# Stage 1 of a hybrid encoder block as a pipeline of 12 units, with inverse roots computed in rows

## The chip, the cores and the metric

The kernel runs on one core of one Trainium2 chip. The metric is device microseconds (us) of one execution, as the median over runs. TensorE (PE) multiplies matrices, VectorE (DVE), ScalarE (ACT) and GpSimd (POOL) work on tiles in SBUF, and SyncE (SP) issues nearly all transfers. Each engine executes its own instructions strictly in order, and waits on semaphores for the others.

## The reference

One layer over 1040 tokens (16 meta tokens and 1024 inputs), width 1024, all in float32:

```python
h = h + hybrid_mixer(rms_norm(h, norm_mix), w_in, ...)   # projections, two branches, gates, output
h = h + conv_ffn(rms_norm(h, norm_ffn), ffn_up, ffn_conv, ffn_down)
# hybrid_mixer, cut:
proj = hn @ w_in                                          # q, k, v, f_logit, rw, gates
qh, kh = rms_norm(q heads), rms_norm(k heads)             # forgetting attention, 8 heads of 64
z = rw + mu * (rw_prev - rw)                              # token shift for the RWKV-7 branch
kk = (kr * k_k) / max(norm per head, 1e-12)               # inverse root
y = rwkv7_scan(r, decay, k, v, -kk, kk * a)               # delta rule, done in 17 chunks of 64 tokens
yn = (y - mean) * rsqrt(var + GN_EPS)                     # per head
g_fox, g_rwkv = split(sigmoid(gates + g_b))
merged = g_fox * (o_fox @ w_bf) + g_rwkv * (o_rwkv @ w_br)
return merged @ w_o
```

## The kernel before, in words

Features lie on the 128 partitions and tokens along the free dimension, so a projection tile is [128 features, up to 384 tokens]. Tokens are cut in three groups `G` (384, 384, 272) in stage 1 and three windows `CW` of 342 later. Large products are split in a high and a low part of reduced float32 (`mm3`, lines 190 to 200: three matmuls per 128-row slice of the contraction); small ones are plain float32, which the records show as two instructions. Weights come through `wload` (L172): a transfer to `wf`, a cast on ACT to `wh`, a subtraction on POOL to `wl`, with `fb` and `wb` places.

An instruction scheduler orders each engine's list at build time: the order in which the source emits instructions is the priority, and an instruction of lower priority can go ahead where the scheduler's model sees the engine free. Tiles with one tag share a fixed number of places (`bufs`); a new tile waits until a place is released.

Stage 0 (`stage0`) loads and normalizes the input per group. Stage 1 (`stage1`) prepares the RWKV branch for four pairs of heads, `p` = 0 to 3. Per pair it emits the projections `zk`, `zr`, `zv` for all three groups (`proj`, `rw_tile`), the low-rank parts (`lora`), three units (`unit(p, c)`, one for each group), and `solve(p)`. A unit is a chain: a scan for the cumulated decay, exponentials, the normalized `kk` (L396 to L410: a block-sum matmul with `bo`, maximum, Ln, Exp, one Newton step of four instructions in `newton_rsqrt`), then `ar` and `bk`, the products `am` (L424) with their mask (L425), transposes of `bk` and `zv`, the bonus term, and stores. `solve` (L253) inverts triangular blocks: 128 instructions of transposing matmuls (L264), 60 dependent DVE steps (L275, L277) with matmuls back (L282), and two small rounds (L294, L301); its result `at` goes to `t_d` in memory. All temporaries and projections of stage 1 share one tag `u` with 28 places.

Gate projections (`gates`, L815) are a generator of 3-matmul steps, 16 weight tiles by three windows by eight steps, which `fill` advances between other work; each is placed behind `S.last_pe`, the last marked matmul on PE. At the end of stage 1 `fill(S, 84)` emits 92 steps. Stage 2 merges attention (`qk_chunk` normalizes queries and keys, one chunk ahead of its use) with the RWKV chain over 17 chunks (`rw_chain`) and, behind it, `group_norm`. Stage 3 multiplies the branches by their output weights and the gates (tanh of stored gate values, L940), stage 4 applies `w_out` and the second norm, stage 5 is the gated MLP.

Inverse roots: stage 0 takes Sqrt on ACT and a reciprocal on rows of tokens; `unit`, `qk_chunk`, `group_norm` and stage 4 work at full width, with the same sum in all rows of a head, by Ln and Exp(-0.5 x) on ACT and (not for queries) `newton_rsqrt`. PSUM tags in stage 1: three banks for projections, two for `aux`, two for `am` and `tp`, one for gates.

Of the kernel before, what the change touches and what calls it, by code (L numbers as in the profile page):

```python
# [7 lines left out]
F32 = mybir.dt.float32  # L8
F32R = mybir.dt.float32r
BF16 = mybir.dt.bfloat16  # L10
AF = mybir.ActivationFunctionType
# [27 lines left out]
NU = 28  # L39
# [15 lines left out]
def constants(S):  # L55
# [10 lines left out]
    S.eps = cp.tile([P, 1], F32, name="eps")  # L66
    nc.vector.memset(S.eps[:], NORM_EPS)
    S.geps = cp.tile([P, 1], F32, name="geps")
    nc.vector.memset(S.geps[:], GN_EPS)
# [3 lines left out]
def constants2(S):  # L73
# [9 lines left out]
    S.a0h = lin("a0", 4, 0.5, 0.0)  # L83
    S.kah = lin("k_a", 4, 0.5, 0.0)
# [17 lines left out]
def stage0(S, p0):  # L102
# [11 lines left out]
    for c, (t0, t1) in enumerate(G):  # L114
# [7 lines left out]
        else:  # L122
            tl = [U("xt") for _ in range(KD)]
# [6 lines left out]
    def stats(c):  # L130
# [12 lines left out]
        blk = [(a, min(P, n - a)) for a in range(0, n, P)]  # L143
        for j, (a, m) in enumerate(blk):
            for k in range(na):
                nc.tensor.matmul(ps[:m, j:j + 1], lhsT=sq[k][:, a:a + m], rhs=S.ones[:, 0:1], start=k == 0, stop=k == na - 1)
        r = p0.tile([P, 3], F32, name="r", bufs=2)
        for j, m in ((slice(0, 2), P), (slice(2, 3), blk[2][1])):
            nc.scalar.activation(out=r[:m, j], in_=ps[:m, j], func=AF.Sqrt, bias=S.eps[:m])
            nc.vector.reciprocal(out=r[:m, j], in_=r[:m, j])  # L150
        ps = psum(S, "tp")
        for j, (a, m) in enumerate(blk):
            nc.tensor.matmul(ps[:, a:a + m], lhsT=r[:m, j:j + 1].broadcast_to([m, P]), rhs=S.ident[:m, :m], start=True, stop=True)
# [18 lines left out]
def wload(S, src, kt, pool=None, tag="w", fb=3, wb=4):  # L172

    nc = S.nc
    pool = pool or S.wp
    res = []
# [130 lines left out]
def stage1(S):  # L307
    nc, tc = S.nc, S.tc
    with tc.tile_pool(name="p1", bufs=1) as p1:
        U = lambda name: p1.tile([P, 390], F32, name=name, tag="u", bufs=NU)  # L310
        v3 = lambda t, nc_: t[:, :64 * nc_].rearrange("p (c t) -> p c t", t=64)
# [3 lines left out]
        tc.keep_in_program_order(nc.scalar.preload_act_table_set("sqrt_and_others"))  # L315
# [8 lines left out]
        for c in stage0(S, p1):  # L324
# [6 lines left out]
            zk0.append(U("zk"))  # L331
# [6 lines left out]
        def proj(p, i):  # L338
            w = wload(S, S.A["w_rw"][2 + 3 * p + i], KD)
            z = []  # L340
            for c, (t0, t1) in enumerate(G):
                z.append(U(("zk", "zr", "zv")[i]))
                rw_tile(S, p1, 2 + 3 * p + i, z[c][:, :t1 - t0], w, c)
            pads(z[2])
            return z

        def lora(p, c):
# [3 lines left out]
            sw, tha = U("sw"), U("tha")  # L351
            ps = psum(S, "aux")
            nc.tensor.matmul(ps[:, :n], lhsT=lup[0:64, pc], rhs=wa[0:64, t0:t1], start=True, stop=True)
            with tc.issue_after(S.last_exp.ins) if p else nullcontext():
                nc.scalar.activation(out=sw[:, :n], in_=ps[:, :n], func=AF.Tanh, scale=0.5, bias=S.w0h[:, p:p + 1])
            ps = psum(S, "aux")
            nc.tensor.matmul(ps[:, :n], lhsT=lup[64:128, pc], rhs=wa[64:128, t0:t1], start=True, stop=True)
            with tc.issue_after(S.last_exp.ins) if p else nullcontext():
                S.th = nc.scalar.activation(out=tha[:, :n], in_=ps[:, :n], func=AF.Tanh, scale=0.5, bias=S.a0h[:, p:p + 1])
# [10 lines left out]
        def unit(p, c, zk, zr, zv, sw, tha, at):  # L370
# [18 lines left out]
            with tc.issue_after(S.ld.ins):  # L389
# [15 lines left out]
            if c == 2:  # L405
                nc.gpsimd.memset(inv[:, n:N], 1.0)
# [769 lines left out]
```

## Time and profile before

| | |
|---|---|
| median of 3 runs (range) | 2078.41 us (2077.85 to 2081.44) |
| profiled execution | 2079.23 us, span 2077.4 us, mean granted PE clock 0.954 |
| busy PE, PE weight loads | 1944.7 us, 1735.0 us |
| busy DVE, ACT, POOL | 901.8 us, 774.1 us, 563.7 us |

Busy times are of the profiled execution. In rows by stretch the columns are: start and end in us, length, then busy us and instruction count of PE, PE's weight loads, DVE, ACT and POOL, then the granted clock as a share of full speed, the busy share of the DMA engines and GB/s. In rows of waits: who waited, for whom, total us, times, longest. In rows of groups: line, engine, operation, tiles, shapes, count, busy us, mean ns, idle time before them. In rows of the timeline and the chain: start, duration, engine and line.

### The profile page before, as it was taken

Reading aid. Unit: us, or ns where it says so; the run is one execution under the profiler, and the core shown is the slowest. Engines: PE = TensorE matmul, PEld = TensorE weight load, DVE = VectorE, ACT = ScalarE, POOL = GpSimd, SP = SyncE. Lnnn points to the kernel's source line nnn. Section 1 sums busy time; section 2 is a strip of 40 time slices with the busy share of each in tenths; the row PEclk is TensorE's granted clock in tenths of the full one; section 3 lists DMA queues with packets and bytes.
Section 4 is the critical chain, followed back from the end, with each engine's and each line's share of the span. In section 5 each row is a group of like instructions: output and inputs, shape, how many; then the busy total and the mean of one; then the engine's idle time right before and its main releaser. Section 6 shows DMA issues by size and latency. Waiting matters only on the chain.

```text
span 2077.4 us, 34698 instructions
## 1 busy us (share of the span) xinstructions
PE 1944.7 (94%) x13800; PEld 1735.0 (84%) x13800; DVE 901.8 (43%) x1797; ACT 774.1 (37%) x1658; POOL 563.7 (27%) x614
## 2 busy tenths in 40 slices
PE   6969696996999999989989999899999999999999
PEld 5948575885888888877877999799898998999997
DVE  5156565554334244167343544843233332333333
ACT  5423242431454354267444534533132231322321
POOL 5311111120320131143221233533232232332322
PEclk9969797996999999999989999999999999999999
DMA  4131414141443233223102533211111111111112
GB/s 151 62 106 43 124 36 128 36 144 52 142 122 92 88 114 106 65 77 97 43 28 84 163 119 112 91 56 47 36 56 51 36 51 51 41 56 47 41 47 101
DMA packets 129489, 163.22 MB, mean 79 GB/s; under 512 B 20272, under 2 KB 87008, under 8 KB 129072
## 3 DMA queue, kind: packets, MB, share of 16 engines
q1 hardware_dynamic: 129072, 160.94, 25.5%
q8 instruction: 109, 1.79, 0.4%
q14 instruction: 52, 0.43, 0.1%
q0 software_dynamic: 256, 0.07, 0.0%
HBM read 117.49 MB, written 43.47 MB: 77 GB/s over the span
## 4 chain that ended last, share of the span: by engine, by line
PE 86%; DVE 7%; ACT 3%; DMA 2%; issue 1%; POOL 0%; SPq 0%; DVEq 0%; ACTq 0%; POOLq 0%
PE mm L196 15%; PE mm L198 15%; PE mm L197 15%; PE dn L196 4%; PE dn L198 4%; PE dn L197 4%; PE gate L196 3%; PE gate L197 3%; PE gate L198 3%; PE t L775 2%; PE o L789 2%; PE am L424 2%; PE s L740 1%; PE am L282 1%; PE s L741 1%
## 5 line engine op out<-in xcount | busy, mean ns | idle before, releaser
L184 POOL TENSOR_TENSOR wl<-wf,wh 128x512 fp32r<-128x512 f32 (+1 forms) x268 | 346.6, 1295 | 794.4 <-ACT wh L183 767.5
L197 PE MATMUL mm<-x,wh 128*128 128x344 f32 (+1 forms) x1056 | 339.1, 321 | 0.0
L196 PE MATMUL mm<-x,wh 128*128 128x344 f32 (+1 forms) x1056 | 337.6, 320 | 1.1 <-DVE ug L1014 1.0
L198 PE MATMUL mm<-x,wl 128*128 128x344 f32 (+1 forms) x1056 | 337.4, 320 | 1.0 <-POOL wl L184 1.0
L183 ACT CAST wh<-wf 128x512 fp32r<-128x512 f32 (+1 forms) x268 | 164.0, 613 | 379.5 <-PE dn L197 185.2
L196 PE MATMUL mm<-xh,wh 128*128 128x386 f32 (+5 forms) x624 | 211.2, 340 | 2.7 <-ACT xh L164 1.3
L198 PE MATMUL mm<-xh,wl 128*128 128x386 f32 (+5 forms) x624 | 210.2, 337 | 0.0
L197 PE MATMUL mm<-xl,wh 128*128 128x386 f32 (+5 forms) x624 | 209.4, 336 | 0.0
L196 PEld LDWEIGHTS mm<-x,wh 128*128 128x128 f32 x1056 | 199.2, 189 | 1.9 <-ACT uv L1012 1.2
L198 PEld LDWEIGHTS mm<-x,wl 128*128 128x128 f32 x1056 | 199.0, 189 | 1.7 <-POOL wl L184 1.6
L197 PEld LDWEIGHTS mm<-x,wh 128*128 128x128 f32 x1056 | 199.3, 189 | 0.4
L196 PE MATMUL gate<-xh,wh 128*128 128x342 f32 x384 | 139.4, 363 | 2.9 <-ACT sg L829 2.8
L1041 DVE TENSOR_TENSOR h<-h,dn 128x512 f32<-128x512 f32 x96 | 66.1, 689 | 168.9 <-PE dn L198 168.4
L198 PE MATMUL dn<-gh,wl 128*128 128x512 f32 x352 | 138.8, 394 | 0.0
L196 PE MATMUL dn<-gh,wh 128*128 128x512 f32 x352 | 138.6, 394 | 0.0
L197 PE MATMUL dn<-gl,wh 128*128 128x512 f32 x352 | 138.6, 394 | 0.0
L196 PEld LDWEIGHTS mm<-xh,wh 128*128 128x128 f32 x624 | 120.8, 194 | 10.0 <-issue 3.6
L197 PEld LDWEIGHTS mm<-xl,wh 128*128 128x128 f32 x624 | 120.9, 194 | 5.0 <-issue 1.6
L198 PEld LDWEIGHTS mm<-xh,wl 128*128 128x128 f32 x624 | 120.5, 193 | 5.3 <-issue 2.3
L198 PE MATMUL gate<-xh,wl 128*128 128x342 f32 x384 | 124.3, 324 | 0.0
L197 PE MATMUL gate<-xl,wh 128*128 128x342 f32 x384 | 124.2, 323 | 0.0
L1013 DVE SCALAR_TENSOR_TENSOR uv<-mm,par,uv 128x342 f32<-128x342 f32 (+1 forms) x66 | 37.8, 573 | 162.6 <-ACT uv L1012 162.6
(309 smaller groups left out, 3790.6 us busy)
## 6 DMA issues: line engine op xcount, KB each, us to landing
wf<-in_w_up_dram SPq DMA_DIRECT2D x88, 256.0 KB, 2.5
am<-am_d SPq DMA_DIRECT2D x17, 512.0 KB, 5.0
sg_d<-sg SPq DMA_DIRECT2D x48, 171.0 KB, 2.5
sg<-sg_d SPq DMA_DIRECT2D x48, 171.0 KB, 3.0
wf<-in_w_gate_dram SPq DMA_DIRECT2D x32, 256.0 KB, 2.8
wf<-in_w_out_dram SPq DMA_DIRECT2D x32, 256.0 KB, 2.9
wf<-in_w_down_dram SPq DMA_DIRECT2D x32, 256.0 KB, 2.7
am_d<-am SPq DMA_DIRECT2D x20, 384.0 KB, 2.9
```

What stands on the lines that cost most here:

```text
L183: nc.scalar.copy(out=wh[:, :n], in_=wf[:, :n])
L184: nc.gpsimd.tensor_tensor(out=wl[:, :n], in0=wf[:, :n], in1=wh[:, :n], op=ALU.subtract)
L196: nc.tensor.matmul(ps, lhsT=wh, rhs=xh, start=first and k == 0, stop=False)
L197: nc.tensor.matmul(ps, lhsT=wh, rhs=xl, start=False, stop=False)
L198: ins = nc.tensor.matmul(ps, lhsT=wl, rhs=xh, start=False, stop=last and k == n - 1)
L282: nc.tensor.matmul(ps[32 * k:32 * k + 32, n * t:n * t + n], lhsT=x[:nl, :, t0 + t], rhs=S.ident[:nl, 64 * k:64 * k + n], start=True, stop= ...
L424: nc.tensor.matmul(ps[:, j * P:(j + 1) * P], lhsT=bk[r, b0 + j, :], rhs=ar[r, b0 + j, :], start=True, stop=True)
L740: nc.tensor.matmul(ps, lhsT=q1[e][:, qs], rhs=k1[e][:, a:z], start=True, stop=False)
L775: S.last_pe = nc.tensor.transpose(ps[:r, (2 * j + e) * 116:(2 * j + e) * 116 + nq], pb[e][i][:nq, k:k + r], S.ident[:nq, :nq])
L789: S.last_pe = nc.tensor.matmul(po[64 * e:64 * e + 64, :nq], lhsT=vt[:r, kb, 64 * e:64 * e + 64], rhs=pt[:r, 2 * j + e, :nq], start=kb == 0 ...
L1013: nc.vector.scalar_tensor_tensor(out=t[:, :n], in0=ps[:, 1:1 + n], scalar=cw(1), in1=t[:, :n], op0=ALU.mult, op1=ALU.add)
L1041: nc.vector.tensor_tensor(out=hs, in0=hs, in1=ps[:], op=ALU.add)
```

## The change

Stage 1 is emitted as 12 units. Projections and LoRA are done per unit (`proj(p, c)`, `lora(p, c)`), one unit ahead of `unit(p, c)`; the three weight tiles of a pair are held over its three units; `solve(p - 1)` is emitted behind the first unit of pair `p`. Projections and LoRA tiles get a tag of their own, `z`, with 10 places; `u` keeps 15. The shifted projection is built in place, without `zt`. Orderings for ACT's table sets are dropped.

All inverse roots go through `rsqrt_rows`: sums are taken with the tile as stationary operand, so that tokens lie on partitions and the result has one or two columns per block of up to 128 tokens; a first guess from the bits of the float and four Newton steps run on these few columns; matmuls with the identity spread the result over the head's rows, into the same PSUM bank, from which it is read. Ln and Exp of all roots go away, the Sqrt of stage 0 too.

The gates take their tanh when they are stored, not in stage 3. The weight pool is opened three times (stage 1 with `wb` = 6, stage 2 with 4, from stage 3 on again); the last opens after the pool of the gates is closed. Three gate weight tiles, not four, use the common pool.

```diff
@@ stage1 @@
-        for p in range(NP_):
-            zk = proj(p, 0) if p else zk0
-            zr = proj(p, 1)
-            lo = [lora(p, c) for c in range(3)]
-            with tc.issue_after(S.th.ins):
-                S.ld = nc.scalar.preload_act_table_set("natural_log_exp_and_others")
-            zv = proj(p, 2)
-            at = p1.tile([64, 2 * NCH, 64], F32, name="at", bufs=2)
-            for c in range(3):
-                unit(p, c, zk[c], zr[c], zv[c], *lo[c], at)
-            solve(S, p1, p, at)
+        steps = [(p, c) for p in range(NP_) for c in range(3)]
+        def ahead(p, c):
+            return proj(p, c), lora(p, c)
+        ats = {}
+        nxt = ahead(0, 0)
+        for i, (p, c) in enumerate(steps):
+            (z, lo) = nxt
+            if c == 0:
+                ats[p] = p1.tile([64, 2 * NCH, 64], F32, name="at", bufs=2)
+            unit(p, c, *z, *lo, ats[p])
+            if c == 0 and p:
+                solve(S, p1, p - 1, ats[p - 1])
+            if i + 1 < len(steps):
+                nxt = ahead(*steps[i + 1])
+        solve(S, p1, NP_ - 1, ats[NP_ - 1])
...
+        def proj(p, c):
+            t0, t1 = G[c]
+            if c == 0:
+                S.wz = [wload(S, S.A["w_rw"][2 + 3 * p + i], KD) for i in range(1 if p == 0 else 0, 3)]
+            z = [zk0[c]] if p == 0 else []
+            for i in range(len(z), 3):
+                z.append(Z(("zk", "zr", "zv")[i]))
+                rw_tile(S, p1, 2 + 3 * p + i, z[i][:, :t1 - t0], S.wz[i - (p == 0)], c)
...
@@ unit @@
-            nc.tensor.matmul(ps[:, :n], lhsT=S.bo[:], rhs=kk[:, :n], start=True, stop=True)
-            inv = U("inv")
-            tn = U("tn")
-            ss = U("ss")
-            nc.vector.tensor_scalar(out=ss[:, :n], in0=ps[:, :n], scalar1=1e-24, scalar2=None, op0=ALU.max)
-            with tc.issue_after(S.ld.ins):
-                nc.scalar.activation(out=inv[:, :n], in_=ss[:, :n], func=AF.Ln)
-                S.last_exp = nc.scalar.activation(out=inv[:, :n], in_=inv[:, :n], func=AF.Exp, scale=-0.5)
-            newton_rsqrt(nc, inv[:, :n], ss[:, :n], 0.0, tn[:, :n])
+            inv = psum(S, "aux")
+            rsqrt_rows(S, p1, inv, [kk], n, S.bo[:, 0:P:64], 2, floor=1e-24)
...
+def rsqrt_rows(S, pool, ps, sq, n, ind, w, eps=None, floor=None):
+    nc = S.nc
+    nb = -(-n // P)
+    while n % nb:
+        nb += 1
+    m = n // nb
+    o = 496
+    for j in range(nb):
+        for i, q in enumerate(sq):
+            nc.tensor.matmul(ps[:m, o + w * j:o + w * j + w], lhsT=q[:, j * m:j * m + m], rhs=ind, start=i == 0, stop=i == len(sq) - 1)
+    W = w * nb
+    vt, yt, tt = [pool.tile([P, 8], F32, name=nm, bufs=2) for nm in ("rv", "ry", "rt")]
+    v, y, t = vt[:m, :W], yt[:m, :W], tt[:m, :W]
...
+    nc.vector.tensor_scalar(out=y.bitcast(I32), in0=v.bitcast(I32), scalar1=-0.5, scalar2=1597463007.0, op0=ALU.mult, op1=ALU.add)
+    for _ in range(4):
+        nc.vector.tensor_tensor(out=t, in0=v, in1=y, op=ALU.mult)
+        nc.vector.scalar_tensor_tensor(out=t, in0=t, scalar=-0.5, in1=y, op0=ALU.mult, op1=ALU.mult)
+        nc.vector.scalar_tensor_tensor(out=y, in0=t, scalar=1.5, in1=y, op0=ALU.add, op1=ALU.mult)
+    for j in range(nb):
+        for i in range(w):
+            r = P // w
+            l = yt[:m, w * j + i:w * j + i + 1].broadcast_to([m, r])
+            nc.tensor.matmul(ps[i * r:(i + 1) * r, j * m:(j + 1) * m], lhsT=l, rhs=S.ident[:m, :m], start=True, stop=True)
...
@@ qk_chunk (keys and queries), and alike in group_norm and stage4 @@
-    nc.tensor.matmul(pm[:, :n], lhsT=S.bo64[:], rhs=sq[:, :n], start=True, stop=True)
-    r = ap.tile([P, 348], F32, name="rq", bufs=1)
-    nc.scalar.activation(out=r[:, :n], in_=pm[:, :n], func=AF.Ln, bias=S.eps[:])
-    nc.scalar.activation(out=r[:, :n], in_=r[:, :n], func=AF.Exp, scale=-0.5)
-    if newton:
-        newton_rsqrt(nc, r[:, :n], pm[:, :n], NORM_EPS, ap.tile([P, 348], F32, name="rq2", tag="sq", bufs=1)[:, :n])
-    nc.vector.scalar_tensor_tensor(out=raw[:, :n], in0=raw[:, :n], scalar=gain, in1=r[:, :n], op0=ALU.mult, op1=ALU.mult)
+    rsqrt_rows(S, ap, pm, [sq], n, S.bo64[:, 0:P:64], 2, eps=NORM_EPS)
+    nc.vector.scalar_tensor_tensor(out=raw[:, :n], in0=raw[:, :n], scalar=gain, in1=pm[:, :n], op0=ALU.mult, op1=ALU.mult)
...
@@ gates, stage3 @@
-            nc.scalar.activation(out=sg[:], in_=ps[:, :342], func=AF.Identity, bias=S.par("gate_b", m))
+            nc.scalar.activation(out=sg[:], in_=ps[:, :342], func=AF.Tanh, scale=0.5, bias=S.gbh[:, m:m + 1])
...
-                nc.scalar.activation(out=sg[:], in_=sg[:], func=AF.Tanh, scale=0.5)
...
@@ build @@
-        S.wp = ctx.enter_context(tc.tile_pool(name="w", bufs=1))
         with tc.tile_pool(name="gp", bufs=1) as S.gp:
-            with tc.tile_pool(name="ps1", bufs=1, space=PSUM) as S.pp:
+            S.wb = 6
+            with tc.tile_pool(name="w1", bufs=1) as S.wp, tc.tile_pool(name="ps1", bufs=1, space=PSUM) as S.pp:
...
-            with tc.tile_pool(name="ps2", bufs=1, space=PSUM) as S.pp:
+            S.wb = 4
+            with tc.tile_pool(name="w2", bufs=1) as S.wp, tc.tile_pool(name="ps2", bufs=1, space=PSUM) as S.pp:
                 stage2(S)
+        S.wp = ctx.enter_context(tc.tile_pool(name="w3", bufs=1))
```

More of the change, by code (lines that the diff above doesn't have):

```diff
@@ L38 @@
 G = [(0, 384), (384, 768), (768, 1040)]
-NU = 28
+NU = 15
+NZ = 10
 _PCOLS = {}
@@ L122, in stage0 @@
         else:
-            tl = [U("xt") for _ in range(KD)]
+            tl = [U("xt") if c == 1 else p0.tile([P, 384], F32, name="xt", tag="z", bufs=NZ) for _ in range(KD)]
             for k in range(KD):
@@ L142, in stats @@
         ps = psum(S, "aux")
[L143 to L153, printed above, removed]
+        rsqrt_rows(S, p0, ps, sq[:na], n, S.ones[:, 0:1], 1, eps=NORM_EPS)
         return ps
@@ L169, in stage0, with wload @@
         yield c
-def wload(S, src, kt, pool=None, tag="w", fb=3, wb=4):
+def wload(S, src, kt, pool=None, tag="w", fb=3, wb=None):
     nc = S.nc
     pool = pool or S.wp
+    wb = wb or S.wb
     res = []
@@ L247, in rw_tile @@
     mm3(S, ps[:, :n + 2], w, xwin(S, t0, n + 2), mark=True)
-    t = pool.tile([P, 384], F32, name="zt", bufs=2)
-    nc.scalar.activation(out=t[:, :n], in_=ps[:, 2:2 + n], func=AF.Identity, scale=mu1)
-    nc.vector.scalar_tensor_tensor(out=z, in0=ps[:, 1:1 + n], scalar=mu, in1=t[:, :n], op0=ALU.mult, op1=ALU.add)
+    nc.scalar.activation(out=z, in_=ps[:, 2:2 + n], func=AF.Identity, scale=mu1)
+    nc.vector.scalar_tensor_tensor(out=z, in0=ps[:, 1:1 + n], scalar=mu, in1=z, op0=ALU.mult, op1=ALU.add)
 def solve(S, p1, p, at):
@@ L664, in attention @@
         n = t1 - t0
-        kn = qk_chunk(S, ap, wk, S.par("kg"), t0, t1, True)
+        kn = qk_chunk(S, ap, wk, S.par("kg"), t0, t1)
         for e in range(2):
@@ L791, in q_block @@
             yield 1.0
-    lb = ap.tile([P, 116], F32, name="lb", tag="rq", bufs=1)
+    lb = ap.tile([P, 116], F32, name="lb", bufs=1)
     nc.scalar.copy(out=lb[:, :nq], in_=po[:, 128:128 + nq])
@@ L858, in group_norm @@
             ps = psum(S, "gn")
-            nc.tensor.matmul(ps[:, :342], lhsT=S.bo64[:], rhs=sq[:], start=True, stop=True)
-            r = T("r", 2)
-            nc.scalar.activation(out=r[:], in_=ps[:, :342], func=AF.Ln, bias=S.geps[:])
-            nc.scalar.activation(out=r[:], in_=r[:], func=AF.Exp, scale=-0.5)
-            newton_rsqrt(nc, r[:], ps[:, :342], GN_EPS, sq[:])
-            nc.vector.tensor_tensor(out=y[:], in0=y[:], in1=r[:], op=ALU.mult)
+            rsqrt_rows(S, op, ps, [sq], 342, S.bo64[:, 0:P:64], 2, eps=GN_EPS)
+            nc.vector.tensor_tensor(out=y[:], in0=y[:], in1=ps[:, :342], op=ALU.mult)
             nc.scalar.activation(out=y[:], in_=y[:], func=AF.Identity, scale=S.par("gn_w", p), bias=S.par("gn_b", p))
@@ L994, in stage4 @@
                 st = psum(S, "st")
-                nc.tensor.matmul(st[:, :342], lhsT=S.ones[:], rhs=acc[c][:], start=True, stop=True)
+                rsqrt_rows(S, p4, st, [acc[c][:]], 342, S.ones[:, 0:1], 1, eps=NORM_EPS)
                 norm(c, st)
```

64 lines of the change are left out of this document (24 added, 40 removed).

## The prediction

> **What bounds the kernel now.** I read the 40 slices of the page first, then busy time by stage, then the waits of TensorE, then single rows for prices.
>
> ```profile
> PE   6969696996999999989989999899999999999999
> DVE  5156565554334244167343544843233332333333
> PEclk9969797996999999999989999999999999999999
> ```
>
> A slice is 52 us. TensorE (PE) is busy 9 tenths or more from slice 11 on, nearly without a break; the holes lie in the first ten, and in the same slices the granted clock falls. So stage 1 is the loose stage and all that follows is bound by PE. The stretches below give busy us (and counts) of PE, PE's weight loads, DVE, ACT and POOL, then the granted clock:
>
> ```profile
> 47.00:104.00 57.00, 57.00 (x333) 52.17 (x332) 11.29 (x21) 26.03 (x53) 24.48 (x35) 1.00 0.18 56
> 104.00:156.50 52.50, 33.07 (x154) 24.25 (x154) 29.41 (x51) 12.67 (x27) 8.55 (x16) 0.64 0.36 109
> 156.50:258.90 102.40, 85.18 (x727) 67.62 (x728) 59.01 (x127) 34.40 (x65) 18.20 (x32) 0.83 0.27 81
> 258.90:361.40 102.50, 85.47 (x727) 67.33 (x726) 59.24 (x127) 34.56 (x65) 17.87 (x32) 0.83 0.27 81
> 424.50:477.00 52.50, 47.82 (x310) 42.29 (x312) 24.32 (x41) 18.09 (x38) 13.74 (x20) 1.00 0.47 145
> 477.00:526.00 49.00, 30.62 (x433) 23.35 (x433) 23.59 (x66) 9.54 (x19) 4.18 (x12) 0.62 0.21 55
> 600.00:850.00 250.00, 248.56 (x2494) 211.96 (x2493) 92.87 (x223) 105.32 (x266) 45.67 (x47) 1.00 0.35 103
> ...
> PE am L424 <- DVE bk L415: 37.4, 7, 8.1
> PE am L282 <- DVE x L277: 11.8, 26, 1.0
> ```
>
> 47 to 104 us: projections, dense at full clock. 104 to 156.5: the three units of head pair 0, a chain of small steps on DVE; PE waits and its clock drops to 0.64. One head pair then costs 102.4 us, with the clock at 0.83. From 424.5 the units of pair 3 run with gate matmuls between them at full clock, and from 477 the last solve runs alone. PE's longest wait (37.4 us) is for `bk` (L415), the end of the unit's DVE chain. From 600 on PE is full, DVE and ACT below half.
>
> **The change, part by part.** Durations are those of the profiled execution: 2079.2 us, span 2077.4, so 1.8 us lie around the span; it stands 0.8 us above the median of 2078.4, and the sum is made against 2079.2. Differences under about 0.2% (4 us) can't be told from no change here.
>
> *What one head pair holds.* Rows for prices (start, duration, line):
>
> ```profile
> 104.02 0.34 PE L196 MATMUL mm<-xh,wh 128*128 128x386 f32 x1
> 104.19 0.34 PE L197 MATMUL mm<-xl,wh 128*128 128x386 f32 x1
> 110.03 0.29 PE L198 MATMUL mm<-xh,wl 128*128 128x274 f32 x1
> 110.16 0.29 PE L196 MATMUL mm<-xh,wh 128*128 128x274 f32 x1
> ...
> 1285.43 0.74 PE L995 MATMUL st<-acc,ones 128*128 128x342 f32 x2
> L859 PE MATMUL gn<-sq,bo 128*128 128x342 f32 x24 | 9.2, 467 | 1.6 <-ACT sq L857 1.5
> ...
> 424.47 1.19 PE am L424 x12
> 447.88 1.19 PE am L424 x12
> 470.11 1.19 PE am L424 x12
> ...
> 166.03 1.37 PE am L282 x40
> 203.60 2.14 PE am L294 x64
> 210.11 2.14 PE am L301 x64
> 258.92 4.04 PE am L264 x128
> 476.99 4.06 PE am L264 x128
> 515.33 4.32 DMA t_d<-at
> ```
>
> Matmuls overlap, so the step between starts counts, not the duration: 0.17 us at 386 columns, 0.13 at 274. A pair's nine projection tiles are 144 x 0.172 + 72 x 0.128 = 34 us. A plain f32 matmul shows as two instructions: 0.74 for both, 0.45 to 0.47 for one, so 0.28 to 0.29 each, 0.58 together or 1.7 ns a column. LoRA (3120 columns) 5.3 us, the two block sums (2080) 3.5, 26 transposes of 128 columns 5.7, 34 `am` products at 1.19 for six 6.7, the solve 4.0 + 128 x 1.37/40 + 2.1 + 2.1 = 12.6. Together 68 us at full clock, in a period of 102.4; DVE holds 59 of it. So about 34 us a pair are waits and low clock.
>
> *The pipeline of 12 units.* Projections and LoRA of the next unit are emitted between units, and `solve(p-1)` after the first unit of pair p. What a unit costs when PE has filler is on record: the `am` rows of pair 3, 424.47, 447.88, 470.11, are 23.4 and 22.2 us apart, with gates as filler (17.5 without, 52.5/3). In the new order the filler is 13 us of projection and LoRA, and a third of a solve, which holds DVE for 7 us a unit (L275 and L277 below: 44.2 + 40.4 over 12 units). The PE floor is 68/3 plus the new row sums, 23.3; the unfilled chain plus the solve's DVE share gives 17.5 + 7 to 8 = 25. I take 25.5 for the nine units of pairs 1 to 3 and 20 for pair 0, where no solve is pending. The first unit starts earlier than 104, because four projection tiles (2 x 24 x (0.172 + 0.128) = 14.4) and two thirds of the LoRA (3.3) move behind it: 86. Its tiles need places that the last input tiles hold; these are used up by the normalization before 47, so that wait costs nothing. Units end at 86 + 60 + 229.5 = 375.5. The last solve took 38.3 us (476.99 to 515.33) and stays exposed to stage 2; with gates between its matmuls I take 40. The 92 steps of gate work that are emitted behind stage 1 (three matmuls of 342 columns each, 3 x 0.172 x 342/386 = 0.46, so 42 us) now lie beside the last unit and this solve rather than beside pair 3's units: hidden either way. `t_d` is then stored at 416, not 515.3: **-99 us**. Bounds: at the PE floor everywhere 86 + 52.5 + 210 + 38 = 387, so -129; if the solve and next projections do not overlap the chain, 31 us a unit and 23 for pair 0, 86 + 69 + 279 + 42 = 476, so -39. The likelier end is the nearer to the recorded 23 us.
>
> *Inverse roots with tokens on partitions*, 51 calls outside stage 0 (12 units, 24 in `qk_chunk`, 12 in `group_norm`, 3 in stage 4). Out goes one f32 matmul of 342 to 384 columns, Ln and Exp on ACT and, but for the 12 query chunks, four full-width DVE steps. In come sums in rows, 14 tiny DVE steps in a chain, and six broadcasts of 64 output rows.
>
> ```profile
> 633.89 0.58 PE L789 MATMUL o<-apt,avt 128*64 128x116 f32 x7
> L763 PE MATMUL o<-ident,linv x144: 259/264/313, 595.0 to 1124.6; 116*64 116x116 f32 x128, 112*64 112x112 f32 x16
> 33.57 1.28 PE L146 MATMUL aux<-ones,sq 128*128 128x1 f32 x10
> 161.80 0.19 DVE L275 TENSOR_TENSOR xm<-x 98x30 f32<-98x30 f32 x1 [3.23 <-ACT x L268]
> 162.02 0.19 DVE L277 TENSOR_TENSOR x<-x,xm 98x30 f32<-98x30 f32 x1
> L275 DVE TENSOR_TENSOR xm<-x 98x30 f32<-98x30 f32 (+14 forms) x120 | 44.2, 368 | 18.2 <-ACT x L268 14.5
> L277 DVE TENSOR_TENSOR x<-x,xm 98x30 f32<-98x30 f32 (+14 forms) x120 | 40.4, 336 | 4.2
> L614 DVE TENSOR_TENSOR inv<-inv,tn 128x384 f32<-128x384 f32 (+1 forms) x12 | 7.4, 614 | 0.7
> L402 ACT ACTIVATE inv<-ss 128x384 f32<-128x384 f32 (+1 forms) x12 | 5.9, 492 | 15.0 <-DVE ss L400 15.0
> ```
>
> L763 is the same broadcast; alternating halves (L789, seven in 0.58, one lasting 0.26) step by 0.053 us, so 12 instructions are 0.64. Six sum instructions at 0.1 (L146: (1.28 - 0.25)/9) are 0.6. That is 1.24 for 0.58: +0.66 us of PE a call. Tiny dependent DVE steps start 0.22 apart, 14 make 3.1 us; what goes is five steps near 0.55 (2.6) and two ACT steps of 0.5. So DVE and the unit's chain stay as they are, within 0.5 us, and this is in the 25.5 above. In stage 2 nothing covers PE: 36 x 0.66 = **+24 us**. Bounds: 0, if the loose issue in stage 2 takes it, and +54 (broadcasts without pairing 12 x 0.117 + 0.68 - 0.58 = 1.5 each). The query chunks' DVE chain is new (12 x 3.1 over 600 us, DVE under 40% busy) and is hidden by the chunk being one ahead.
>
> On this the Trainium skill speaks the other way. "Perfetto Trace Analysis", Identifying the Most-Contended Engine, says that busy time of matmuls is a bad measure, and weight-load share the better one. Here weight loads hold 212 of 250 us in the 600 to 850 row; by that page 38 us are free there, the +24 would be 0 and the sum 24 lower. I stay with the starts, which leave no such gap.
>
> *Weight pools split into three.* The pool of stage 3 opens where the gates' pool lay, and its first weights wait for the last gate matmul:
>
> ```profile
> wf<-in_w_out_dram SPq DMA_DIRECT2D x32, 256.0 KB, 2.9
> L184 POOL TENSOR_TENSOR wl<-wf,wh 128x512 fp32r<-128x512 f32 (+1 forms) x268 | 346.6, 1295 | 794.4 <-ACT wh L183 767.5
> L183 ACT CAST wh<-wf 128x512 fp32r<-128x512 f32 (+1 forms) x268 | 164.0, 613 | 379.5 <-PE dn L197 185.2
> ```
>
> Landing 2.9, cast 0.6, subtract 1.3, hops: 5 to 6 us, queued behind it on SP only later loads. **+6**, bounds 0 (addresses do not meet) and +12 (the same at the start of stage 2). *Stage 4*: a table load and two ACT steps go from the chain into the first normalized tile, 14 tiny steps come: **-1**, bounds -3 and +2. Tanh of the gates moves from stage 3 to the gates, six weight slots for four, tiles without `zt`: ACT is far from full there, 0.
>
> Sum: -99 + 24 + 6 - 1 = -70, so 2079.2 - 70 = **2009 us**.
>
> **The rivals.** *Better pipeline*: stage 1 near its PE floor and stage 2 absorbing the sums: -115 + 5 + 3 = -107, 1972. For it: pair 3 ran at full clock with filler. Against: the solve keeps DVE for 21 of 70 us. *The units stay in step*: ten `z` places hold two units, and the solve's DVE chain holds up evictions; 30 us a unit or more, gaps remain, the clock stays near 0.83 as in 156.5 to 258.9: -55 + 25 + 6, 2055. "TensorE: Matmul & The Clock Gate" of the Trainium skill, Part 1, says an idle window halves the clock until work is sustained; the 0.64 and 0.62 rows agree in direction. *Slower*: PE issues in order, and in each of the 51 calls broadcasts stand behind the 3.1 us chain; where nothing is put between, all later matmuls wait. At 3.1 exposed each, 158 us: 2167. It decides once over 70/51 = 1.4 us a call stay exposed. Against it: between L629 and its use the trace of before has other matmuls on PE.
>
> **How the numbers follow.** My forecast 0.60 (own range 1975 to 2035), better pipeline 0.14, units in step 0.16, slower 0.07, and 0.03 for a loss that just cancels the gain. Leaving out most of the slow case and the far end of the good one gives 1962 to 2058. Faster 0.90, same 0.03, slower 0.07.
>
> **What would show it.** Right: the clock at 0.95 or more from 90 to 375 us, `am` groups (L424) of successive units 22 to 28 us apart, `t_d` of the last pair near 416, PE's wait for `bk` gone from the top. Stage 2 takes some 24 us more between its first chain matmul and the first branch matmul. Wrong: waits of PE for the tiny Newton tile high in the list, or clock holes left in stage 1.

## The result and the profile after

The changed kernel takes 2151.49 us (median of 4 runs, 2147.29 to 2155.28) against 2078.13 us for the kernel before in the same comparison (4 runs, 2076.54 to 2081.44): a ratio of 1.035, with a 95% interval of 1.0325 to 1.0375. The forecast was 2009 us, with a range of 1962 to 2058. It was wrong in sign: 73 us slower, not 69 us faster. The profiled execution of the changed kernel took 2147.29 us, with a span of 2145.5 us.

The slices of the changed kernel, to be laid beside those of before:

```profile
PE   5989888986999999989979899999999999999999
DVE  6345464545354254166453453753233232332333
PEclk9997797895999999989979999999999999999999
```

A slice is now 54 us. TensorE's holes in the first ten slices are still there, and so is the low clock (in five of slices 4 to 10). The holes at slices 18 and 21, in the tail of stage 2, were there before as well; the second is deeper now (7 for 8), and the one at slice 23 is new. The stretches of the changed kernel (same columns as before) are cut at its units and at the joints of the stages. Each row stands for itself; some overlap.

```profile
0.00:542.70 542.70, 449.57 (x3640) 382.44 (x3640) 276.50 (x708) 156.97 (x324) 122.43 (x217) 0.84 0.28 87
103.90:177.40 73.50, 61.38 (x373) 50.68 (x372) 36.31 (x89) 21.82 (x46) 17.43 (x30) 0.92 0.32 102
177.40:287.80 110.40, 95.91 (x780) 78.79 (x779) 57.86 (x154) 27.54 (x57) 17.83 (x32) 0.76 0.25 76
287.80:396.10 108.30, 95.16 (x801) 79.39 (x801) 59.12 (x154) 27.25 (x57) 17.62 (x31) 0.83 0.24 72
485.20:542.70 57.50, 38.34 (x462) 28.83 (x462) 26.07 (x71) 10.92 (x22) 5.53 (x15) 0.57 0.23 61
542.70:903.00 360.30, 355.29 (x3637) 313.88 (x3637) 146.76 (x439) 137.60 (x339) 71.84 (x75) 1.00 0.34 99
903.00:1199.00 296.00, 257.64 (x1992) 220.41 (x1989) 151.99 (x573) 114.62 (x298) 66.35 (x66) 0.90 0.17 51
```

Three units of a pair still take 108 to 110 us (rows 3 and 4), against 102.4 before, at clocks of 0.76 and 0.83. The last solve stays exposed at 0.57. The last two rows are stage 2: its part with the RWKV chain, and the tail behind that. The same two parts in the kernel before:

```profile
526.00:877.00 351.00, 348.50 (x3422) 302.97 (x3422) 128.74 (x296) 147.49 (x362) 72.43 (x75) 1.00 0.35 101
877.00:1127.00 250.00, 231.76 (x1580) 193.58 (x1580) 134.41 (x306) 134.60 (x343) 70.80 (x69) 0.95 0.20 61
```

Where the 68.1 us between the two profiled executions (2147.3 and 2079.2) arise, by the first start of the matmuls named:

| part | before, us | after, us | difference |
|---|---|---|---|
| start to the first matmul of the RWKV chain | 526.0 | 542.7 | +16.7 |
| stage 2, part with the chain | 351.0 | 360.3 | +9.3 |
| stage 2, tail up to the first branch matmul | 250.0 | 296.0 | +46.0 |
| stage 3 | 96.8 | 92.3 | -4.5 |
| stage 4, and stage 5 up to the first `dn` matmul | 218.5 | 219.1 | +0.6 |
| stage 5 from its first `dn` matmul | 635.1 | 635.1 | 0 |

The waits of TensorE over the whole span of the changed kernel:

```profile
PE am L271 <- DVE x L266: 16.4, 40, 1.1
PE aux L609 <- DVE sq L140: 15.9, 2, 15.3
PE mm L186 <- DVE zk L239: 11.4, 8, 1.8
PE o L627 <- DVE ry L622: 9.8, 4, 4.3
PE aux L627 <- DVE ry L622: 9.3, 4, 4.9
PE mm L186 <- ACT wh L173: 9.0, 2, 8.4
PE gn L627 <- DVE ry L622: 6.3, 3, 3.5
```

The wait for `bk` (37.4 us before) is gone. In its place stand waits for the last Newton step (`ry`, L622; 9.8 + 9.3 + 6.3 = 25.4 us), for the eviction of a projection (`zk`, L239), and one of 8.4 us for the first weights of stage 3. The waits of DVE in stage 1, 86 to 545 us, tell more:

```profile
DVE am L408 <- PE am L407: 62.4, 29, 12.3
DVE kk L393 <- PE aux L627: 36.2, 12, 4.9
DVE bon L428 <- PE aux L426: 31.7, 12, 5.3
DVE rv L616 <- PE aux L609: 23.7, 10, 4.5
```

Two of them were there before: the third (33.2 us) and the wait for the products (L407), which was 47.5 us and is now 14.9 us longer, with a longest of 12.3 us for 4.9. New are the waits for the broadcasts (L627) and for the row sums (L609), 59.9 us together; the one visit of the old root cost DVE 6.9 us (its maximum, L400, behind the block sum). The chain of waits of the changed kernel, its `am` rows cut to one for most units, with what stands between two units where a solve comes:

```profile
103.89 1.00 PE am L407 x12
...
177.43 1.59 PE am L407 x9
...
186.25 4.03 PE am L253 x122
...
229.41 3.23 PE am L290 x61
232.64 4.61 PE am L407 x22
...
263.14 1.00 PE am L407 x12
...
287.77 0.87 PE am L407 x9
...
340.08 4.60 PE am L407 x22
...
396.08 1.19 PE am L407 x12
...
463.99 1.32 PE am L407 x11
...
485.22 1.63 PE am L407 x9
```

Units without a solve between them follow each other by 21 to 31 us (263.14 to 287.77: 24.6), 25.7 on average; units around a solve by 55.2 us (177.43 to 232.64), 52.3 us (287.77 to 340.08) and 67.9 us (396.08 to 463.99). The mean is (485.22 - 103.89)/11 = 34.7 us, where 25.5 and 20 were forecast. The products of the unit at 232.64 start at the very end of the solve's last round (229.41 + 3.23 = 232.64), although their input was long done, and so it is with those at 463.99, by DVE's timeline:

```profile
218.30 0.55 DVE L398 SCALAR_TENSOR_TENSOR bk<-kk,ei 128x384 f32<-128x384 f32 x1
...
440.82 0.55 DVE L398 SCALAR_TENSOR_TENSOR bk<-kk,ei 128x384 f32<-128x384 f32 x1
```

The solve's rounds and the units' products and transposes (`am`, `tp`) share two PSUM banks, and banks are handed out in the order of the source. There the solve stands ahead of the next unit. So the solve, meant to run beside the units, holds them up. The `t_d` rows of the four pairs, first and last start:

```profile
L293 SPq DMA_DIRECT2D t_d<-at x4: 451/452/457, 233.3 to 531.4; - x4
```

The last is at 531.4; 416 was forecast, and 515.3 was the time before.

### The profile page after: what moved, and what is told of

Read it like the earlier page. It is cut to its first block, busy times and chain, and to the rows that moved or that the text cites. A ratio compares the mean times of both kernels' runs of the same rounds, so it can differ in the third digit from the quotient of the medians.

```text
span 2145.5 us, 36826 instructions
## 1 busy us (share of the span) xinstructions
PE 1999.7 (93%) x14676; PEld 1803.9 (84%) x14676; DVE 948.0 (44%) x2377; ACT 687.0 (32%) x1488; POOL 562.3 (26%) x615
## 4 chain that ended last, share of the span: by engine, by line
PE 85%; DVE 7%; issue 3%; ACT 3%; DMA 1%; POOL 0%; SPq 0%; ACTq 0%; POOLq 0%; DVEq 0%
PE mm L186 15%; PE mm L187 15%; PE mm L188 15%; PE dn L186 4%; PE dn L188 4%; PE dn L187 4%; PE gate L186 3%; PE gate L187 3%; PE gate L188 3%; PE t L783 2%; PE o L797 2%; PE am L407 1%; PE s L748 1%; PE s L749 1%; PE ch L499 1%
## 5 line engine op out<-in xcount | busy, mean ns | idle before, releaser
L186 PEld LDWEIGHTS mm<-xh,wh 128*128 128x128 f32 x624 | 125.5, 202 | 24.8 <-DVE zk L239 15.5
L187 PEld LDWEIGHTS mm<-xl,wh 128*128 128x128 f32 x624 | 125.4, 201 | 2.0 <-issue 1.0
L188 PEld LDWEIGHTS mm<-xh,wl 128*128 128x128 f32 x624 | 124.9, 200 | 1.4 <-issue 0.5
```

Of the source, the lines that this page charges most:

```text
L186: nc.tensor.matmul(ps, lhsT=wh, rhs=xh, start=first and k == 0, stop=False)
L187: nc.tensor.matmul(ps, lhsT=wh, rhs=xl, start=False, stop=False)
L188: ins = nc.tensor.matmul(ps, lhsT=wl, rhs=xh, start=False, stop=last and k == n - 1)
```

## Experiments

All times are medians; ratios are to the kernel before on the same chip, with their 95% interval. "Last `t_d`" is the figure at the end of stage 1 (531.4 in the changed kernel), and stage 2 is counted from the first RWKV chain matmul to the first branch matmul (601.0 us before, 656.3 after). The theories were: the solve's bank turns hold the units up; too few `z` places do; the root inside the unit does, since its two visits to TensorE stand behind projections; and, for stage 2, the row roots' TensorE work alone against broadcasts that stand behind the tiny chain.

**The solve on a bank of its own.** One of the three projection banks is given to it.

```diff
-        ps = psum(S, "am")          # four times in solve
+        ps = psum(S, "sv")
-                banks(S, mm="0 1 2", aux="3 4", am="5 6", tp="5 6", gate="f")
+                banks(S, mm="0 1", aux="3 4", am="5 6", tp="5 6", sv="2", gate="f")
```

> The changed kernel, but solve has a PSUM bank of its own (one taken from the projections, which keep two); before this, solve and the units' am and tp tiles share two banks. Theory A (banks): in the changed kernel each of the three solves emitted between units holds the two banks for about 40 us, and the next unit's am products wait; here the unit behind a solve falls from 52 to 55 us to about 30, the last t_d store moves from 531 to about 465, and the time from 2151 to about 2090. Theory B (too few z places) and theory C (the chain of the row roots): no gain, 2145 to 2160, since the units are held up by other things and the projections lose a bank.

2118.59 us, 1.0198 (1.0182 to 1.0214); last `t_d` 506.1, stage 2 657.0. So a bank of its own gains 25 us of stage 1, net of the projection bank that it takes away; 66 were expected. The units now come evenly, (447.56 - 104.68)/11 = 31.2 us apart by the starts of their products, and DVE's wait for the products falls from 62.4 to 35.7 us. The gaps around the solves are gone, but the units without a solve, 25.7 us apart in the changed kernel, are now as far apart as the rest. That is still 6 us a unit more than forecast: banks are a part, not the whole.

**More places for projections.**

```diff
-NZ = 10
+NZ = 13
```

(`hs` of the solve shares another tile's place to make room.)

> The changed kernel with 13 places for projections instead of 10 (solve's hs shares the place of x to make room). Theory B (places): with ten, the projections of the next but one unit sit in PSUM until the current unit gives up its tiles; with three more they are evicted at once, units without a solve go from 25 us to about 20, and the time falls by 40 us to about 2110. Theories A (banks) and C (roots): within 10 us of 2151.

2153.7 us, 1.0365 (1.035 to 1.0381); last `t_d` 534.8. Nothing is gained; the theory of the places falls, as far as it goes for the layout with shared banks, the only one in which it was tried.

**The old roots from stage 2 on, stage 1 as changed.** First try:

```diff
-    rsqrt_rows(S, ap, pm, [sq], n, S.bo64[:, 0:P:64], 2, eps=NORM_EPS)
+    nc.tensor.matmul(pm[:, :n], lhsT=S.bo64[:], rhs=sq[:, :n], start=True, stop=True)
+    nc.scalar.activation(out=r[:, :n], in_=pm[:, :n], func=AF.Ln, bias=S.eps[:])
+    nc.scalar.activation(out=r[:, :n], in_=r[:, :n], func=AF.Exp, scale=-0.5)
...        # group_norm and stage 4 likewise; gates' tanh back in stage 3
+    tc.keep_in_program_order(nc.scalar.preload_act_table_set("natural_log_exp_and_others"))
```

> The changed kernel, with the roots of stages 2 to 4 and the gates' tanh put back as they were; stage 1 keeps the pipeline and the row roots. Theory C (row roots cost stage 2: PE work and PE waiting behind the Newton chain): stage 2 shrinks from 656 us by 45 to 50, the time is about 2103. If the 55 us come from the split weight pools or from where stage 1 leaves the gates: 2140 to 2155.

2160.66 us, 1.0405 (1.038 to 1.043). This one missed its aim. Its groups of ACT show why:

```profile
L657 ACT ACT_TABLE_LOAD x22 | 28.2, 1283 | 0.4
L656 ACT ACT_TABLE_LOAD x22 | 28.2, 1283 | 0.8 <-PE o L654 0.4
L886 ACT ACT_TABLE_LOAD x10 | 12.8, 1283 | 0.2
L887 ACT ACT_TABLE_LOAD x9 | 11.5, 1283 | 0.2
```

These are 63 table loads of 1.283 us, one for nearly every Ln and every Exp. A table load at a LoRA function (L355, at 475.39 us) stands behind the preload (at 471.40), and from there nearly every Ln and Exp has a load of its own. So this run says nothing on the row roots. With the preload behind the last Exp of stage 1, and Ln and Exp behind the preload:

```diff
-    tc.keep_in_program_order(nc.scalar.preload_act_table_set("natural_log_exp_and_others"))
+    with tc.issue_after(S.last_exp.ins):
+        S.ld = nc.scalar.preload_act_table_set("natural_log_exp_and_others")
```

> As roots_old_from2 (the changed kernel, with the roots of stages 2 to 4 and the gates' tanh as before), but ACT's Ln and Exp keep one table set: the load is placed behind the last Exp of stage 1. In roots_old_from2 the set changed at every root, 70 loads of 1.28 us in stages 2 to 4. Theory C (row roots cost stage 2 about 50 us): stage 2 comes back to about 610 us (601 and the 8 us wait for weights at the start of stage 3), the time is 2105. Rival (stage 2 is long because of the pools or of the order that stage 1 leaves): stage 2 stays above 640, 2140 or more.

2103.48 us, 1.0108 (1.0091 to 1.0124); last `t_d` 533.3, stage 2 610.6. The two parts of its stage 2:

```profile
544.30:895.20 350.90, 348.41 (x3420) 302.88 (x3421) 129.25 (x296) 147.84 (x363) 72.38 (x75) 1.00 0.35 102
895.20:1154.90 259.70, 232.78 (x1587) 194.96 (x1581) 134.31 (x309) 135.13 (x346) 66.14 (x66) 0.94 0.19 58
```

So row roots cost stage 2 of the changed kernel 656.3 - 610.6 = 46 us: 9.4 in the part with the chain (360.3 against 350.9), 36.3 in the tail (296.0 against 259.7). What is left against before, 9.6 us, lies in the tail, where the 8.4 us wait for weights of the third pool stands.

**Row roots alone, in the old order.** `rsqrt_rows` for all roots in the kernel before, with its order, its tiles and its one weight pool; the gates' tanh is moved and the orderings for ACT's table sets are dropped here too.

```diff
-            nc.tensor.matmul(ps[:, :n], lhsT=S.bo[:], rhs=kk[:, :n], start=True, stop=True)
...
-            newton_rsqrt(nc, inv[:, :n], ss[:, :n], 0.0, tn[:, :n])
+            rsqrt_rows(S, p1, inv, [kk], n, S.bo[:, 0:P:64], 2, floor=1e-24)
...        # and at the other places
```

> The kernel before with the row roots everywhere, the gates' tanh moved and the table orderings dropped, but with the old order of stage 1, the shared tag of 28 places and one weight pool. Theory C: stage 2 is 45 us longer, and each of the twelve units 1 to 3 us longer: about 2078 + 45 + 20 = 2143. If the row roots cost only their PE work as predicted: 2078 + 24 + 8 = 2110. If the loss of stage 2 is due to the pools: 2078 to 2090.

2148.51 us, 1.0331 (1.0309 to 1.0353); last `t_d` 537.2, stage 2 653.9. Row roots, with these two smaller edits, by themselves make nearly the whole loss: +53 in stage 2 and +22 in stage 1 (537.2 against 515.3). The pipeline of units then gains only 6 us (537.2 to 531.4). The 8.4 us wait for weights is absent here.

**What of a row root costs stage 2.** One Newton step for four (nine of the 14 tiny steps go, in stage 1 too; roots are inexact):

```diff
-    for _ in range(4):
+    for _ in range(1):
```

> The changed kernel with one Newton step instead of four in each row root: 5 tiny DVE steps in the chain instead of 14, the rest of the computation unchanged (the roots are less exact). If the length of the chain costs stage 2 its time (PE waits behind it): 36 calls x 9 x 0.2 = 65 us of chain go, stage 2 shrinks by 30 to 40 and stage 1 by 10 to 20, 2105. If the cost is the PE work and the two visits on PE: stage 2 shrinks by less than 12, 2135 to 2145.

2109.03 us (2 runs), 1.0138 (1.0115 to 1.0162); last `t_d` 517.8, stage 2 635.8. Its two parts of stage 2:

```profile
529.10:888.70 359.60, 357.24 (x3637) 313.68 (x3637) 126.17 (x331) 137.45 (x340) 71.86 (x75) 1.00 0.34 99
888.70:1164.90 276.20, 251.19 (x1994) 215.71 (x1990) 123.02 (x357) 114.29 (x298) 65.80 (x67) 0.94 0.19 54
```

The other way round: the 14 tiny steps stay, but on columns of one full-width sum, and their result scales by a partition's value, so that no row sums and no broadcasts are left (what is multiplied is not the root of each token):

```diff
-    rsqrt_rows(S, ap, pm, [sq], n, S.bo64[:, 0:P:64], 2, eps=NORM_EPS)
+    y = chain_only(S, ap, pm, sq[:, :n], n, S.bo64[:], NORM_EPS)   # matmul, 14 steps on ps[:, :6]
...
+    nc.vector.scalar_tensor_tensor(..., scalar=y[:, 0:1], in1=pm[:, :n], ...)
```

> The changed kernel, but in qk_chunk and group_norm (36 calls) the sums are taken by one full-width f32 matmul as before, the 14 tiny DVE steps run on six of its columns, and the result multiplies the tile by a per-partition value beside the sums: no sums in rows, no broadcasts, so these roots are left out. PE has the work and the visits of before, DVE has the new chain. If PE work and visits cost the time: stage 2 falls by 35 to 45 us, 2110. If the DVE chain does: stage 2 falls by less than 15, 2137 to 2150.

2109.67 us (2 runs), 1.0142 (1.0121 to 1.0162); stage 2 620.2:

```profile
543.50:893.10 349.60, 346.54 (x3420) 302.79 (x3421) 146.21 (x440) 137.62 (x340) 72.08 (x75) 1.00 0.36 101
893.10:1163.70 270.60, 234.23 (x1585) 191.57 (x1581) 155.01 (x573) 114.34 (x298) 66.26 (x66) 0.93 0.19 56
```

The two stretches separate the terms. With the chain running (12 calls: by the broadcasts' rows, half of the 24 query and key chunks), fewer Newton steps change nothing (359.6 against 360.3), and taking out sums and broadcasts takes out all of the loss (349.6): there the tiny steps are hidden and only TensorE's work counts, 9.4/12 = 0.78 us a call. In the tail (24 calls: the other half and the 12 of `group_norm`) fewer steps gain 19.8 us (296.0 to 276.2) and taking out sums and broadcasts 25.4 (to 270.6). At 0.78 the TensorE work there is an estimated 19, which leaves 17 to 18 of the 36.3. The waits of TensorE fit that: all 16.1 us for `ry` in stage 2 (9.8 + 6.3 in the list above, seven waits of up to 4.3 us) lie in the tail, none beside the chain. These are broadcasts standing behind the tiny steps, and the matmuls behind these with them. TensorE's busy time in the tail, 257.6 of 296.0 against 232.8 of 259.7, splits it otherwise: 25 us more busy, at a lower clock (0.90 against 0.94), and 11 us more idle. The two gains overlap, so this split is good to some microseconds. Nor do the broadcasts bring the whole loss: without them, but with the tiny steps, 10.9 us stay in the tail (270.6 against 259.7), and TensorE waits there for the tile that these scale instead (8.9 us for `raw`, L660).

**Both cures together.** Bank for the solve, and old roots from stage 2 on (the edits of the first and of the fourth experiment):

> solve_bank (a PSUM bank of its own for solve) and roots_old2 (old roots from stage 2 on) together; stage 1 keeps the pipeline and its row roots. If the two causes are independent: stage 1 ends 25 us sooner than in the changed kernel and stage 2 takes 610 us, so 2151 - 33 - 46 = 2072, about 0.3% below the kernel before. If the gains overlap: 2085 to 2105.

2071.12 us (10 runs), 0.996 (0.9947 to 0.9974); last `t_d` 511.5, stage 2 611.3. The two gains add up (2072 was expected), and now the pipeline is worth something, if little. With the solve on the gates' bank, so that projections keep their three, and the last solve, which has no gates to spare, back on `am`:

```diff
-        ps = psum(S, "am")
+        ps = psum(S, "sv" if p < NP_ - 1 else "am")
-                banks(S, mm="0 1 2", aux="3 4", am="5 6", tp="5 6", gate="f")
+                banks(S, mm="0 1 2", aux="3 4", am="5 6", tp="5 6", sv="f", gate="f")
```

> As comb2 (old roots from stage 2 on, pipeline in stage 1), but the first three solves use the PSUM bank of the gates, which is idle until the end of stage 1, so the projections keep three banks; the last solve, behind which no unit comes, uses the am banks. If the third projection bank matters to the pipeline: stage 1 ends 5 to 15 us before comb2's 511, 2060. If the units are bound by their own chain: 2066 to 2074.

2054.38 us, 0.9893 (0.9867 to 0.9918); last `t_d` 497.2, stage 2 607.8. So the third projection bank is worth 14 us of stage 1 (511.5 to 497.2), and sharing the banks costs 36 (533.3 in roots_old2 to 497.2), more than the 25 of the first experiment. And with two Newton steps in the row roots, which remain in the units and in stage 0, `range(2)` for `range(4)`:

> comb_f with two Newton steps instead of four in the row roots, which remain in stage 0 and stage 1 only: 8 tiny DVE steps in the chain instead of 14, 1.2 us less per unit. newton1 gained 13.6 us in stage 1 with nine steps less, so six steps less give about 9: 9 us below comb_f. If the solve's bank was what made the chain count: within 3 us of comb_f.

2046.91 us, 0.9845 (0.9827 to 0.9862); last `t_d` 483.2, units 29.2 us apart. The 14.0 us that stage 1 gains are what the steps take (12 x 6 x 0.2 = 14.4): in this layout the units wait for these in full. This is the fastest here of the kernels that leave nothing out, 1.5% ahead of the kernel before.

**What remains in stage 1.** From the kernel with the solve on its own bank, once with a solve of one step for 30 (its result is not the inverse), once with the root left out of the units (`kk` is then a scaled product):

```diff
-    for s in range(1, 31):
+    for s in range(1, 2):
```
```diff
-            inv = psum(S, "aux")
-            rsqrt_rows(S, p1, inv, [kk], n, S.bo[:, 0:P:64], 2, floor=1e-24)
-            ... out=kk[:, :n], in0=zk[:, :n], scalar=S.par("k_k", p), in1=inv[:, :n] ...
+            ... out=kk[:, :n], in0=zk[:, :n], scalar=1e-9, in1=kk0[:, :n] ...
```

> solve_bank with the 60 dependent DVE steps of each solve left out but for the first two (the block inverses are not computed). If the solve's DVE work holds up the units, which are 31 us apart in solve_bank: the nine units of pairs 1 to 3 come 5 to 8 us closer, and the last t_d store moves from 506 to 430 to 450 (20 of it in the last solve itself). If the units are bound by their visits to PE: the store moves by the last solve's 20 us and little more, to 480.

> solve_bank with the row root of stage 1's units left out (the normalized kk is replaced by a product of small size): no sums, no Newton chain, no broadcasts in the unit. If the row root and its two visits to PE set the unit: units come 5 to 6 us closer, the last t_d store moves from 506 to about 445. If the projections and the other visits to PE set it: less than 2 us a unit, 485 to 500.

They took 2069.12 and 2044.67 us, one run each. Without the solve's steps the last `t_d` comes at 453.3 (-53, a part of which is the last solve itself, which stands alone), and the units are 27.9 us apart. Without the root it comes at 429.6 (-76.5), and the units are (368.99 - 95.83)/11 = 24.8 us apart, near the forecast spacing; but the forecast had a root in its units, and this kernel has none. Stage 1 without the root:

```profile
0.00:440.20 440.20, 392.68 (x3401) 340.60 (x3401) 254.77 (x539) 154.85 (x322) 125.64 (x216) 0.95 0.35 107
```

The clock is 0.95 where it was 0.84 in the changed kernel and 0.87 in solve_bank. The timelines of the changed kernel show one way in which a root that visits TensorE twice becomes dear. DVE first, then TensorE:

```profile
143.62 0.17 DVE L622 SCALAR_TENSOR_TENSOR ry<-rt,ry 68x8 f32<-68x8 f32 x1
148.69 0.50 DVE L393 SCALAR_TENSOR_TENSOR kk<-zk,par,aux 128x272 f32<-128x272 f32 x1 [4.90 <-PE aux L627]
```
```profile
143.62 0.34 PE L188 MATMUL mm<-xh,wl 128*128 128x386 f32 x1
...
147.68 0.34 PE L187 MATMUL mm<-xl,wh 128*128 128x386 f32 x1
147.95 0.69 PE L627 MATMUL aux<-ident,ry 68*64 68x68 f32 x16
```

The last Newton step ends at 143.79. The broadcasts that spread its result begin at 147.95, behind a queue of projection matmuls that were put ahead of them; DVE stands 4.9 us for that. In solve_bank, the run with the solve's own bank, DVE waits 24.1 us for row sums and 26.4 for broadcasts in stage 1. The chains of tiny steps themselves are longer than 14 x 0.2 = 2.8 us: in the 12 units of solve_bank they take 56.4 us from first step to last, 4.7 each, and in the changed kernel 57.4, 4.8 each. Two things lengthen them. Instructions of the solve go between the steps, and some steps take up to 1.30 us in place of 0.17, as in the first unit of the changed kernel, here with POOL's subtraction for a weight tile:

```profile
93.80 1.28 DVE L621 SCALAR_TENSOR_TENSOR rt<-rt,ry 128x6 f32<-128x6 f32 x1
```
```profile
93.77 1.29 POOL L174 TENSOR_TENSOR wl<-wf,wh 128x512 fp32r<-128x512 f32 x1 [3.56 <-ACT wh L173]
```

The two end within 0.02 us of each other. In the 12 units of the changed kernel 14 of the 168 steps are stretched so, each to the end of such a subtraction, 12.7 us in all. Waits and chains in solve_bank make 107 us, more than the 76.5 that leaving out the root gives back, since DVE does other work between the steps.

**Is it the row root, or any root?** In the best layout (comb_f), the old root with Ln and Exp in the units, and two more places for temporaries:

```diff
-            rsqrt_rows(S, p1, inv, [kk], n, S.bo[:, 0:P:64], 2, floor=1e-24)
+            nc.tensor.matmul(ps[:, :n], lhsT=S.bo[:], rhs=kk[:, :n], start=True, stop=True)
...        # maximum, Ln, Exp, newton_rsqrt, at full width
```

> comb_f with the old root in the units of stage 1 too (block sum at full width, maximum, Ln and Exp on ACT, one Newton step at full width), and two more places for the temporaries; row roots remain in stage 0 alone. Ln and Exp now lie between Tanh and Exp of the units, so ACT loads tables twice a unit, 24 x 1.28 us. If the row root's two visits to PE and its chain of tiny steps are what stretch the unit: units 3 to 5 us closer, less about 2 for the table loads, stage 1 ends 10 to 40 us before comb_f's 497, 2015 to 2045. If any root at this place costs the same: within 10 us of comb_f, 2045 to 2065.

2077.16 us (10 runs), 0.9989 (0.9978 to 0.9999); last `t_d` 502.8, units 30.3 us apart against 30.2. Both expectations missed it: it is 23 us slower than comb_f. Of the 14.2 us between the two profiled executions, 12.3 lie ahead of the first matmul of the RWKV chain (520.8 against 508.5), 5.6 of these ahead of the last `t_d`. The other root buys nothing in the pipeline. But it changes ACT's table set 24 times, since units and LoRA now alternate (groups of ACT of this kernel):

```profile
L396 ACT ACT_TABLE_LOAD x12 | 15.4, 1283 | 0.2
L397 ACT ACT_TABLE_LOAD x12 | 15.4, 1283 | 0.2
```

So its 2.6 us a unit of loads lie in the same chain, and what an old root without these would give was not tried. That the row root is dearer than the old one inside the pipeline is therefore not shown; in the old order it is, with the two smaller edits of rows_only beside it (+22 us in stage 1).

## Why the prediction was wrong, point by point

**Pipeline: -99 forecast, about +16 measured; this is the larger failure.** Two steps of it failed. "Units end at 86 + 60 + 229.5" rests on a unit of 17.5 us without any filler, with the solve's share of DVE on top, and leans on the 23 us of pair 3 of the kernel before, where gates fill TensorE. Gates, a filler that nothing in the unit's chain depends on, do not stand for projections and a solve: with these the units came 34.7 us apart, and 31.2 with the solve on its own bank. Projections are put ahead of the unit's next visit to TensorE (143.79 to 147.95 above), and their evictions go to the chain's own engines; what the evictions cost apart was not measured. The second is "DVE and the unit's chain stay as they are, within 0.5 us, and this is in the 25.5". The forecast priced the 14 steps at 3.1 us and put the waits of two visits to TensorE at nothing; in the changed kernel the steps took 4.8 us a unit and the waits 59.9 us in all, 5 a unit. Of the 115 us between 416 and 531.4 the runs account for 25 (the solve's bank turns, which the forecast had not looked at, net of a projection bank), 76.5 (the root in the unit, left out altogether) and 13.6 that stay open (429.6 to 416). The 76.5 are not all excess of the row root: the forecast's units held a root at 2.6 us of DVE and 1.0 of ACT, 43 us in the 12 units, so some 33 us, by estimate, fall to the second step and the rest to the first. The solve's DVE steps, 53 us by bank_short, lie across these shares and are no further sum. The first unit starts about where it was forecast (86), by its scan on DVE in the changed kernel:

```profile
87.28 0.95 DVE L371 TENSOR_TENSOR_SCAN cs<-smask,sw 128x384 f32<-128x384 bf16 x1
```

But its products come 16.6 us later (103.89), where the kernel before, with its scan at

```profile
101.35 0.95 DVE L379 TENSOR_TENSOR_SCAN cs<-smask,sw 128x384 f32<-128x384 bf16 x1
```

and first products at 114.17, took 12.8: the unit's chain is longer by 3.8 us from the first unit on, with no solve near it. So the start moved by 14.1 us by the scans and by 10.3 by the products, where 18 were forecast. In this unit the 14 steps take 6.0 us, three of them stretched to the end of a subtraction on POOL.

**Row roots in stage 2: +24 forecast, +46 measured.** TensorE's work was well sized: 0.66 us a call forecast, 0.78 measured where the chain hides all else, which would be 28 us for 36 calls. What failed is "hidden by the chunk being one ahead", and with it the weight given to the rival of broadcasts standing behind the chain. While the RWKV chain runs, it holds; in the tail little else is at hand for TensorE, and 17 to 18 us of waiting come on top, 0.7 to 0.8 us a call on average. In the old order and with one weight pool the loss in stage 2 is 53. The slower rival at 0.07 had the right mechanism for the tail at a quarter of its price; it said that 1.4 us exposed a call decide, and in stage 1 about 76.5/12 = 6 us a unit were at stake. Its argument against itself, that other matmuls lie between sum and use, is what in stage 1 makes the wait long.

On the page's rule that the prediction weighed ("Perfetto Trace Analysis" of the Trainium skill, Identifying the Most-Contended Engine), the runs decide against its use here. Before, weight loads held 303 of 351 us in the part with the chain, 48 free by that rule; 12 calls still lengthened this part by 9.4, and taking their matmuls out gave it back. What "TensorE: Matmul & The Clock Gate" of the Trainium skill, Part 1, says of idle windows agrees in direction with 0.57 in the exposed last solve, where TensorE is busy for 38.3 of 57.5 us, and 0.95 in the stage 1 without roots, with 392.7 of 440.2.

**Weight pools: +6 forecast, 8.4 us seen as a wait, 9.6 left in stage 2** with the old roots. Within its bounds of 0 to 12, and the wait is the one that was forecast; it is absent in rows_only, which has one pool. That the 9.6 are this wait and nothing else is not shown.

**Stages 3 and 4: 0 and -1 forecast, -4.5 and +0.6 measured** (the latter up to the first `dn` matmul). The tanh that moved to the gates is not what stage 3 gains from: with the tanh back in stage 3 it takes 94.3 us in roots_old2, 93.0 in comb2 and 92.4 in comb_f, against 96.8 before. The cause stays open. The tiny step was priced at 0.22 us from start to start and takes 0.20 where nothing comes between.

**The rivals.** "The units stay in step" had the clock right (0.84 for 0.83) and half the picture, units in 108 to 110 us a pair. Of its two causes, `z` places fell with z13; the other, the solve's DVE steps, is borne out by bank_short (31.2 to 27.9 us a unit). The signs named for a wrong forecast both came: PE waits for `ry`, and clock holes in stage 1. The signs for a right one failed but for the vanished `bk` wait; stage 2 took 55 us more, not 24.

## What to carry to other kernels

A spacing measured with one filler does not hold for another: ask whether the new filler is queued ahead of the chain's next visit to the same in-order engine, and whether its evictions go to the chain's engines. Before a serial piece is laid beside a pipeline, give it banks of its own, since shared places are handed out in the order of the source. Count each visit of a chain to a busy engine as a wait and not only as work. Cutting full-width work into a chain of tiny steps between two visits to TensorE costs no more than TensorE's work where other matmuls fill TensorE and nothing waits for the result; price it apart for the dense stretch and the tail.

## What the runs showed of the hardware

The chain of tiny steps costs 0.20 us a step from start to start at 6 and at 8 columns (0.16 to 0.17 busy), so 2.8 us for 14 where nothing comes between. Its place decides what it costs the kernel: nothing beside the RWKV chain (359.6 against 360.3 us with nine steps fewer), all of it in the units of comb_f (14.0 us for six steps fewer). A tiny step on DVE that starts during a subtraction of 512 columns on POOL can last until this ends, 1.28 us for 0.17. The root in each unit took the granted clock of all of stage 1 from 0.95 (without it) to 0.87 (with it, both with the solve on its own bank), so the remaining matmuls ran slower as well; without the solve's steps, but with the root, it was 0.93. How much of the 76.5 us is clock and how much is waiting stays open. And a preload of an ACT table set that one function of another set can pass holds nothing: 76 loads in roots_old_from2 against 10 in roots_old2, where only the places of the preload and of the Ln and Exp differ, at 1.283 us each.
